# One encoder layer on one core: loads put in the order of use and ahead of stores, gates fetched a step ahead, half of the embedding's products moved behind the mixer

## The chip, the core and the metric

The kernel runs on one core of a Trainium2 chip. The metric is the device time of one execution in microseconds (us); lower is better. TensorE (PE) multiplies into PSUM, VectorE (DVE) and ScalarE (ACT) empty PSUM and prepare operands, and SyncE (SP) issues DMA transfers. Each engine works through its own list of instructions in order, and waits where an operand isn't there.

## What is computed

One layer of an encoder for 512 prompt tokens and 8 sample streams of 16 tokens, 640 tokens in all, with D = 1024 and float32 data:

```python
x = x + 0.5 * swiglu(rms_norm(x), ffn1_w_in, ffn1_w_out)        # d_ff = 2816
z = rms_norm(x) @ w_in_mix                                       # feeds both mixers and the gates
br_ret = (rms_norm(retention(z)) * silu(rg)) @ w_br_ret          # 4 heads, chunks of 64
br_fox = forgetting_attention(z, cached keys and values) @ w_br_fox   # 8 heads of 64, 1024 cached frames
x = x + (sigmoid(g0) * br_ret + sigmoid(g1) * br_fox) @ w_out
x = x + 0.5 * swiglu(rms_norm(x), ffn2_w_in, ffn2_w_out)
x = x + (p @ w_ple) * sigmoid(rms_norm(x) @ w_ple_gate)          # the per-layer embedding, p has 256 columns
```

Keys, values, logits of forgetting and the new retention states are outputs too.

## The kernel before

Activations are held transposed, 128 channels by 640 tokens. Every float32 operand of a large product is split in two fp32r halves: ACT casts the high half (`hi`, L269 for weights, L291 for activations), DVE subtracts it to get the low half (L270, L292). A product is then three matmuls of 128x128 by 320 (or 256) columns, recorded on L205 (L228 are transposes on PE).

*Feed-forward blocks* (`ffn`). The 22 column blocks of d_ff go in groups of 8, 8 and 6. One step f makes one block: two half loads fill a `raw` tile (L535; two raw tiles in turn), its four quarters a11 to a22 enter a scheme of seven products in place of eight (`Seven`), for which DVE adds quarters to each other in place (L403 to L405, L415). The split weights go through rings of six tiles, `wh` for the high and `wl` for the low halves; only a22 goes to other tiles, `blk` (38 of them), so that it may be prepared early:

```python
            self.as_is = Parts().add(a11), Parts().add(a22, spare)
```

After each group its activations are multiplied by w_out, and x is read from DRAM, added to and written back (L591, L592), or, in the last group, handed to the mixer: its normed halves are made on ACT (L469), and x is put into `spill` (L681).

*Mixer.* The input projection, the gates, the embedding's products and the FoX branch are a list of units (`units`); the attention and retention steps are written out between them, and after each of these `fill(us)` lets the list advance by so many modelled microseconds of matmul work. FILL_R is that number for each of the 52 retention steps (4 heads of 13). For each sample, 1024 cached frames of keys and values come in four transfers of 1 MB into four `kv` tiles: K0, K1, V0, V1. Gates (`zdram`) and attention results (`foxd`) go through DRAM. The embedding's products p @ w_ple are four units in the mixer; `embed_take` copies each PSUM tile (L1414) and stores it to `ple` (L1415), from where the last stage reads it.

*Order.* All loads and stores are issued by SP, in the order in which the program issues them, apart from what a scheduler moves when it builds the program; a load waits there for its tile to come free, a store for its data, and what stands behind waits as well. `load` adds a dependency that keeps a transfer from being put too early. On the other engines the scheduler decides the order too; it is fixed before the run.

*Behind the mixer.* The retention branch (eight outputs, gated by a sigmoid on ACT, L1548, and a multiplication on DVE that empties PSUM, L1553), then W_out with its sum into x (L1566) and the second norm, then the second feed-forward block. L442, L444 and L447 are ACT's copies out of PSUM in the scheme of seven products; L1427 and L1430 are sigmoid and multiplication of the FoX branch; L1281 and L1359 are DVE steps of retention, L1347 its silu.

Of the kernel before, what the change touches and what calls it, by code (L numbers as in the profile page):

```python
# [11 lines left out]
F32R = mybir.dt.float32r  # L12
# [7 lines left out]
P = 128  # L20
D = 1024
KC = D // P
# [21 lines left out]

LEAD = 30.0

FILL_P0, FILL_P1, FILL_S0, FILL_S, FILL_R, FILL_B = 1.76, 1.6, 19.8, 10.0, 2.6, 6.4

SM = {}
_at = 0  # L50
# [81 lines left out]
def kernel(  # L132
# [26 lines left out]
    def blk(shape=(P, T), dt=F32, tag="blk"):  # L159
        n = 1  # L160
        for s in shape[1:]:
            n *= s
        assert n <= T
        return bp.tile(list(shape), dt, tag=tag, name=nm(tag), bufs=slots[tag])

    def big(shape=(P, 2048), dt=F32):
        return bp.tile(list(shape), dt, tag="kv", name=nm("kv"), bufs=NKV)
# [44 lines left out]
    def load(out, in_, lead=LEAD):  # L212

        i = nc.sync.dma_start(out, in_)
        at = clock[0] - lead
        name = next((nm_ for c, nm_ in reversed(issued) if c <= at), None)
        if name is not None:
            after(i, name, "no tile taken too soon")
# [171 lines left out]
    class Seven:  # L390
# [8 lines left out]
        def first(self, spare=False):  # L399

            a11, a12, a21, a22 = self.given
            self.as_is = Parts().add(a11), Parts().add(a22, spare)
            nc.vector.tensor_tensor(a11, a21, a11, op=ALU.add)  # L403
            nc.vector.tensor_tensor(a21, a21, a22, op=ALU.add)
            nc.vector.tensor_tensor(a22, a11, a22, op=ALU.add)  # L405
            return self
# [51 lines left out]
    class Norm:  # L458
# [33 lines left out]
        def square(self, xc):  # L492
            if not self.squares:
                self.acc = blk()
                nc.scalar.activation(self.acc, xc, AF.Square)
            else:
                sq = blk()
                nc.scalar.activation(sq, xc, AF.Square)
                nc.vector.tensor_tensor(self.acc, self.acc, sq, op=ALU.add)
            self.squares.append(xc)  # L500
# [19 lines left out]
        def row_stats(self, dsts):  # L520

            t = 0
            for d in dsts:
                for c in range(0, d.shape[1], P):
                    mm(d[:, c:c + P], self.rtok[:, t:t + 1].to_broadcast([P, P]), ident, True, True, skip_group_check=True)
                    t += 1
            self.rb, at = blk(), 0
            for d in dsts:
                nc.scalar.copy(self.rb[:, at:at + d.shape[1]], d)
                at += d.shape[1]  # L530
# [7 lines left out]
    def ffn(xd, norm, w_in, w_o, done, ahead=None, begun=None):  # L538
        pair0 = 0
        for npair in F_GROUPS:  # L540
            acts, pieces, waiting = [], carve(), []

            def act(q, ah, al):
                for hf, sl in enumerate(HALVES):
                    g = tmp()
                    nc.vector.tensor_tensor(g, q.g[hf], norm.rb[:, sl], op=ALU.mult)
                    nc.scalar.activation(g, g, AF.Silu)
                    nc.vector.tensor_tensor(g, g, q.u[hf], op=ALU.mult)
                    split_x(ah[:, sl], al[:, sl], g)

            fs = range(2 * pair0, 2 * (pair0 + npair))
            if ahead and not pair0:
                for step in ahead:
                    ah, al = next(pieces), next(pieces)
                    acts.append((ah, al))
                    step(lambda q: act(q, ah, al))
                fs = fs[len(ahead):]
            q = (begun or Seven(*quarters(up_raw(w_in, fs[0])))).split()
            begun = None
            for f in fs:  # L560
                ah, al = next(pieces), next(pieces)
                acts.append((ah, al))
                if f == 0:
                    for i in range(3):
                        q.product(i, norm.ops, (0, 1, 2))
                    for i in range(3):
                        q.product(i, norm.ops, (3,))
                for i in range(3 if f == 0 else 0, 7):
                    if f == 1 and not ahead and i == 2:
                        sums = bank("pg")  # L570
                        norm.token_stats(sums[:, :TB])
                    if f == 1 and not ahead and i == 4:
                        b0, b1 = bank("pg"), bank("pg")
                        norm.row_stats([b0, b1[:, :P]])
                    q.product(i, norm.ops)
                waiting.append((q, ah, al))
                if f != fs[-1]:
                    q = Seven(*quarters(up_raw(w_in, f + 1))).split()
                while waiting and f > 0:
                    act(*waiting.pop(0))  # L580
            kc = 2 * npair
            for op in range(KC // 2):
                raw = raw_unit(w_o[2 * pair0 * P:2 * (pair0 + npair) * P, op * 256:(op + 1) * 256], kc, 256)
                for o in range(2):
                    xc = blk()
                    load(xc, xd[2 * op + o], 12.0)
                    ps = pair()
                    gemm_t(ps, split_w(raw[:, :, o * P:(o + 1) * P]), acts)
                    for hf, sl in enumerate(HALVES):
                        t = tmp()  # L590
                        nc.vector.scalar_tensor_tensor(t, ps[hf][:, :H2], 0.5, norm.rb[:, sl], op0=ALU.mult, op1=ALU.mult)  # L591
                        nc.vector.tensor_tensor(xc[:, sl], xc[:, sl], t, op=ALU.add)  # L592
                    if pair0 + npair == sum(F_GROUPS):
                        done(xc)
                    else:
                        nc.sync.dma_start(xd[2 * op + o], xc)
            pair0 += npair
# [539 lines left out]
    class Sample:  # L1137
        def __init__(self, b):
            self.b = b

        def loads(self):
            self.k, self.v = [], []
            for to, cache in ((self.k, cache_k), (self.v, cache_v)):
                rows = cache[0, self.b].rearrange("(p j) h d -> p j (h d)", j=8)
                for j in (0, 4):
                    t = big((P, 4, 512))
                    load(t, rows[:, j:j + 4, :], 60.0)
                    to += [t[:, i, :] for i in range(4)]

        def step(self, n):  # L1150

# [259 lines left out]
    def embed_take(q):  # L1411
# [4 lines left out]

        return take

    def fox_begin():
        for pr in range(4):  # L1420
            fox_x.append(parts(fetch(foxd[pr]), blk(dt=F32R), blk(dt=F32R)))

    def fox_take(n0):
        def take(ps, o, hf):
            if hf == 0:
                g = fetch(zdram[Z_G1 + n0 + o])
                nc.scalar.activation(g, g, AF.Sigmoid)  # L1427
                ys.append(g)
            g, sl = ys[n0 + o], HALVES[hf]
            nc.vector.tensor_tensor(g[:, sl], g[:, sl], ps[:, :H2], op=ALU.mult)  # L1430

        return take
# [27 lines left out]
        units[-1].done = lambda hd=hd: ready.add(("rg", hd))  # L1460
    units += units_s(Z_G1, O_ZG + D, 8) + units_s(Z_G0, O_ZG, 8)
    units[-1].begin = embed_begin
    units += [Unit("n", w_ple[0][:, q * 256:(q + 1) * 256], embed_take(q), x=p_x) for q in range(4)]
    units[-2].begin = fox_begin
    ys = []
    units += [Unit("t", w_br_fox[0][:, n * P:n * P + 256], fox_take(n), x=fox_x) for n in range(0, KC, 2)]
    feed = run_units(units)

    credit = [0.0]
# [31 lines left out]
                    fill(FILL_P0 if hu == 0 else FILL_P1)  # L1501
    samples = [Sample(b) for b in range(NB)]
    defer(0.0, sample_new)
    samples[0].loads()
    fill(FILL_B)
    for b in range(NB):
        if b + 1 < NB:
            defer(2.0, samples[b + 1].loads)
        for n in range(8):
            samples[b].step(n)  # L1510
            fill((FILL_S if b else FILL_S0) / 8)
# [28 lines left out]

    y_x, pieces = [], carve()
    ret_x = [parts(fetch(retd[n]), blk(dt=F32R), blk(dt=F32R)) for n in range(KC)]
    for op in range(KC // 2):
        raw = raw_unit(w_br_ret[0][:, op * 256:(op + 1) * 256], KC, 256)
        for o in range(2):
            n = 2 * op + o
            g = fetch(zdram[Z_G0 + n])
            nc.scalar.activation(g, g, AF.Sigmoid)  # L1548
            ps = pair()
            gemm_t(ps, split_w(raw[:, :, o * P:(o + 1) * P]), ret_x)  # L1550
            y = ys[n]
            for hf, sl in enumerate(HALVES):
                nc.vector.tensor_tensor(g[:, sl], g[:, sl], ps[hf][:, :H2], op=ALU.mult)  # L1553
            nc.vector.tensor_tensor(y, y, g, op=ALU.add)
            y_x.append(parts(y, next(pieces), next(pieces)))
    norm2 = Norm(2)
    for op in range(KC // 2):
# [13 lines left out]
        norm2.add_pair(*two)  # L1571
        for xc in two:
            norm2.square(xc)

    norm3 = Norm(3)

# [72 lines left out]
```

## Time and profile before

| | |
|---|---|
| median of 3 runs | 1685.03 us (1680.42 to 1686.94) |
| the profiled execution | 1679.24 us |
| its span, first to last instruction | 1677.5 us |
| TensorE busy | 1644.2 us, 98% |
| VectorE, ScalarE busy | 1177.6 us (70%), 740.4 us (44%) |
| data moved | 248.66 MB, mean 148 GB/s |

The profiled execution is one run with the hardware profiler on; its span leaves out what lies ahead of the first instruction and behind the last. Busy shares are means over stages of very different kinds, so they do not say where an engine waits.

### The profile page before, as it was taken

To read this page: it belongs to the slowest core of one execution; us is meant where nothing else is said; L and a number is where in the kernel's file an instruction comes from. 1 tells how busy PE (TensorE), PEld (TensorE's weight loads), DVE (VectorE), ACT (ScalarE), POOL (GpSimd) and SP (SyncE) were. 2 spreads that over 40 slices of the span, in tenths; PEclk is the share of its full clock that TensorE was granted. 3 is DMA by queue.
4 is the path that set the end of the run, shared out by engine and by line. 5 is a ranking of instruction groups with operands and counts; after the bars stand their busy time and mean duration, and the time that the engine had idled before them with its cause. 6 is when DMAs were issued, how large, how long until landed. Compare 5 with 4: busy or idle time off the path is not lost.

```text
span 1677.5 us, 30453 instructions
## 1 busy us (share of the span) xinstructions
PE 1644.2 (98%) x12073; PEld 1573.0 (94%) x12073; DVE 1177.6 (70%) x2524; ACT 740.4 (44%) x1504; POOL 1.4 (0%) x6
## 2 busy tenths in 40 slices
PE   8999999999999999999999999999999999999999
PEld 7999999999999998888789888899999999999998
DVE  5884787577687746677688866657886588568663
ACT  5552354244455545444434445435553255235442
POOL 0000000000000000000000000000000000000000
PEclk9999999999999999999999999999999999999999
DMA  7134324432542234577774679625234332533343
GB/s 240 51 124 147 107 77 131 154 92 90 164 137 90 86 114 142 205 275 260 270 233 158 223 234 309 230 81 163 81 86 159 121 98 84 171 104 97 112 135 92
DMA packets 228574, 248.66 MB, mean 148 GB/s; under 512 B 15280, under 2 KB 195920, under 8 KB 224336
## 3 DMA queue, kind: packets, MB, share of 16 engines
q1 hardware_dynamic: 228224, 246.64, 45.5%
q8 instruction: 95, 1.56, 0.4%
q14 instruction: 47, 0.39, 0.1%
q10 hardware_dynamic: 208, 0.08, 0.0%
HBM read 198.04 MB, written 48.65 MB: 147 GB/s over the span
## 4 chain that ended last, share of the span: by engine, by line
PE 84%; DMA 8%; DVE 4%; ACT 2%; issue 1%; SPq 0%; ACTq 0%; DVEq 0%
PE pa L205 64%; PE pg L205 16%; PE pa L228 4%; DMA raw<-in_ffn_w_in_dram 3%; DMA blk<-xd 2%; DMA blk<-zdram 1%; DVE wl L270 1%; ACT wh L269 1%; DMA out_dram<-kv 1%; DMA kv<-in_cache_fox_k_dram 1%; DMA blk<-foxd 1%; DMA blk<-in_c_rope_dram 0%; PE pg L228 0%; DVE blk L592 0%; DVE kv L1268 0%
## 5 line engine op out<-in xcount | busy, mean ns | idle before, releaser
L205 PE MATMUL pa<-blk,wh 128*128 128x320 f32 x2672 | 580.1, 311 | 12.4 <-ACT wh L269 5.4
L269 ACT CAST wh<-raw 128x512 fp32r<-128x512 f32 (+1 forms) x566 | 338.3, 613 | 514.9 <-PE pa L205 334.8
L205 PEld LDWEIGHTS pa<-blk,wh 128*128 128x128 f32 x2672 | 440.6, 188 | 21.2 <-ACT wh L269 7.3
L270 DVE TENSOR_TENSOR wl<-raw,wh 128x512 fp32r<-128x512 f32 (+1 forms) x566 | 378.4, 680 | 105.8 <-ACT wh L269 100.2
L205 PE MATMUL pa<-blk,wl 128*128 128x320 f32 x1336 | 393.0, 308 | 0.0
L205 PE MATMUL pa<-kv,wh 128*128 128x320 f32 x1344 | 252.6, 308 | 0.0
L205 PEld LDWEIGHTS pa<-blk,wl 128*128 128x128 f32 x1336 | 246.7, 188 | 0.0
L205 PEld LDWEIGHTS pa<-kv,wh 128*128 128x128 f32 x1344 | 211.1, 188 | 0.0
L205 PE MATMUL pg<-blk,wh 128*128 128x320 f32 x768 | 178.4, 318 | 2.5 <-DVE blk L1430 0.9
L205 PE MATMUL pa<-kv,wl 128*128 128x320 f32 x672 | 153.8, 308 | 0.0
L205 PE MATMUL pg<-wh,blk 128*128 128x256 f32 x768 | 149.7, 290 | 1.5 <-ACT tmp L1414 1.5
L205 PEld LDWEIGHTS pg<-blk,wh 128*128 128x128 f32 x768 | 127.5, 188 | 13.3 <-issue 6.7
L205 PEld LDWEIGHTS pg<-wh,blk 128*128 128x128 f32 x768 | 120.2, 188 | 6.4 <-issue 3.0
L205 PE MATMUL pg<-blk,wl 128*128 128x320 f32 x384 | 119.2, 310 | 0.0
L205 PEld LDWEIGHTS pa<-kv,wl 128*128 128x128 f32 x672 | 112.5, 188 | 0.0
L205 PE MATMUL pg<-wl,blk 128*128 128x256 f32 x384 | 110.0, 287 | 0.0
L591 DVE SCALAR_TENSOR_TENSOR tmp<-pa,blk 128x320 f32<-128x320 f32 x96 | 42.7, 485 | 66.8 <-PE pa L205 66.8
L205 PE MATMUL pa<-wh,blk 128*128 128x256 f32 (+1 forms) x432 | 84.2, 289 | 3.2 <-ACT blk L469 1.8
L205 PE MATMUL pa<-blk,blk 128*128 128x320 f32 (+2 forms) x572 | 87.1, 300 | 0.0
L205 PEld LDWEIGHTS pa<-blk,blk 128*128 128x128 f32 (+1 forms) x572 | 77.4, 179 | 1.3 <-issue 0.6
L205 PEld LDWEIGHTS pg<-wl,blk 128*128 128x128 f32 x384 | 72.3, 189 | 2.5 <-issue 1.7
L205 PEld LDWEIGHTS pg<-blk,wl 128*128 128x128 f32 x384 | 72.2, 188 | 1.4 <-issue 1.4
(257 smaller groups left out, 2112.5 us busy)
## 6 DMA issues: line engine op xcount, KB each, us to landing
raw<-in_ffn_w_in_dram SPq DMA_DIRECT2D x88, 512.0 KB, 4.1
raw<-in_w_in_mix_dram SPq DMA_DIRECT2D x25, 1024.0 KB, 6.5
raw<-in_ffn_w_out_dram SPq DMA_DIRECT2D x16, 1024.0 KB, 5.2
kv<-in_cache_fox_k_dram SPq DMA_DIRECT2D x16, 1024.0 KB, 8.5
kv<-in_cache_fox_v_dram SPq DMA_DIRECT2D x16, 1024.0 KB, 6.5
xd<-blk SPq DMA_DIRECT2D x48, 320.0 KB, 2.9
blk<-xd SPq DMA_DIRECT2D x48, 320.0 KB, 5.7
zdram<-blk SPq DMA_DIRECT2D x32, 320.0 KB, 2.4
```

Source lines behind the costliest of these rows:

```text
L205: i = nc.tensor.matmul(out, lhsT, rhs, start=start, stop=stop, **kw)
L228: tick(nc.tensor.transpose(out, in_, ident[: in_.shape[0], : in_.shape[0]]), 0.11)
L269: nc.scalar.copy(hi, src)
L270: nc.vector.tensor_tensor(lo, src, hi, op=ALU.subtract)
L591: nc.vector.scalar_tensor_tensor(t, ps[hf][:, :H2], 0.5, norm.rb[:, sl], op0=ALU.mult, op1=ALU.mult)
```

## The change

Six edits; the work on the engines stays the same but for two more loads of an activation table on ACT.

1. `ffn` loads x two outputs ahead instead of right ahead of its product.
2. The quarter a11 also goes to `blk` tiles instead of the wh and wl rings. Squares and the row factor of the second norm go to `att` tiles instead of `blk`, and the second block takes its norm's sums in step 0 instead of step 1.
3. The loads of the samples are issued in the order K0 of the next sample, V0 and V1 of this one, K1 of the next; before, all four of the next sample stood together.
4. foxd and the gates of the FoX branch are fetched one unit ahead, and their sigmoid is taken at the start of a unit; the same for the gates of the retention branch.
5. Two of the embedding's four units move from the mixer to the place between W_out and the second block.
6. FILL_R falls from 2.6 to 2.45.

```diff
-FILL_P0, FILL_P1, FILL_S0, FILL_S, FILL_R, FILL_B = 1.76, 1.6, 19.8, 10.0, 2.6, 6.4
+FILL_P0, FILL_P1, FILL_S0, FILL_S, FILL_R, FILL_B = 1.76, 1.6, 19.8, 10.0, 2.45, 6.4
...
-            self.as_is = Parts().add(a11), Parts().add(a22, spare)
+            self.as_is = Parts().add(a11, spare), Parts().add(a22, spare)
...
-                sq = blk()
+                sq = att(shape=(P, T))
...
-            self.rb, at = blk(), 0
+            self.rb, at = blk(tag="att" if self.n == 2 else "blk"), 0
...
-                    if f == 1 and not ahead and i == 2:
+                    if f == 0 and i == 3:
                         sums = bank("pg")
                         norm.token_stats(sums[:, :TB])
-                    if f == 1 and not ahead and i == 4:
+                    if f == 0 and i == 6:
...
+            def fetch_x(n):
+                if n < KC:
+                    coming.append(blk())
+                    load(coming[-1], xd[n], 12.0)
+
+            fetch_x(0)
+            fetch_x(1)
             for op in range(KC // 2):
...
-                    xc = blk()
-                    load(xc, xd[2 * op + o], 12.0)
                     ps = pair()
                     gemm_t(ps, split_w(raw[:, :, o * P:(o + 1) * P]), acts)
+                    fetch_x(2 * op + o + 2)
+                    xc = coming.pop(0)
...
+        def loads(self, then):
+
+            if then:
+                then.load(then.k, cache_k)
+            self.load(self.v, cache_v)
+            self.load(self.v, cache_v)
+            if then:
+                then.load(then.k, cache_k)
...
+    def fox_fetch():
+        fox_x.extend(fetch(foxd[pr]) for pr in range(4))
+
     def fox_begin():
         for pr in range(4):
-            fox_x.append(parts(fetch(foxd[pr]), blk(dt=F32R), blk(dt=F32R)))
+            fox_x[pr] = parts(fox_x[pr], blk(dt=F32R), blk(dt=F32R))
+
+    def gates_fetch(n0):
+
+        if n0 < KC:
+            ys.extend(fetch(zdram[Z_G1 + n0 + o]) for o in range(2))
+
+    def gates_begin(n0):
+        for g in ys[n0:n0 + 2]:
+            nc.scalar.activation(g, g, AF.Sigmoid)
+        gates_fetch(n0 + 2)
...
-    units += [Unit("n", w_ple[0][:, q * 256:(q + 1) * 256], embed_take(q), x=p_x) for q in range(4)]
-    units[-2].begin = fox_begin
+    units += [Unit("n", w_ple[0][:, q * 256:(q + 1) * 256], embed_take(q), x=p_x) for q in range(2)]
+    units[-2].begin = fox_fetch
+    units[-1].begin = lambda: gates_fetch(0)
+    units[-1].middle = fox_begin
...
-        if b + 1 < NB:
-            defer(2.0, samples[b + 1].loads)
+        defer(2.0, lambda: samples[b].loads(samples[b + 1] if b + 1 < NB else None))
...
+    gates = [fetch(zdram[Z_G0 + n]) for n in range(2)]
     for op in range(KC // 2):
         raw = raw_unit(w_br_ret[0][:, op * 256:(op + 1) * 256], KC, 256)
+        for g in gates:
+            nc.scalar.activation(g, g, AF.Sigmoid)
+        g2 = gates
+        gates = [fetch(zdram[Z_G0 + 2 * op + n]) for n in (2, 3)] if op < 3 else []
         for o in range(2):
             n = 2 * op + o
-            g = fetch(zdram[Z_G0 + n])
-            nc.scalar.activation(g, g, AF.Sigmoid)
...
+    raw = raw_unit(w_ple[0][:, 512:], 2, 512)
+    w = [Parts().add(raw[:, :, q * 256:(q + 1) * 256]) for q in range(2)]
+    for q in range(2):
+        for t in range(TB):
+            ps = bank("pg")
+            gemm_n(ps[:, :256], w[q], p_x, t)
+            embed_take(q + 2)(ps, t)
```

*ACT in the first feed-forward block.* `raw_383` holds the weights of one step and `raw_406` those of the next; `blk` and `wh` tiles named from them are their high halves. Before:

```order
L269 CAST wh_384_2329<-raw_383_2326 128x512
L291 CAST kv_352_2085<-tmp_375_2223 128x320
L291 CAST kv_352_2085<-tmp_374_2217 128x320
L442 COPY tmp_379_2256<-pa_378_2243 128x320
L269 CAST blk_409_2476<-raw_406_2469 128x512
L269 CAST wh_388_2340<-raw_383_2326 128x512
L269 CAST wh_390_2344<-raw_383_2326 128x512
```

Of the change:

```order
L269 CAST blk_407_2472<-raw_406_2469 128x512
L291 CAST kv_352_2085<-tmp_375_2223 128x320
L444 COPY tmp_380_2257<-pa_377_2230 128x320
L269 CAST wh_388_2340<-raw_383_2326 128x512
L269 CAST wh_390_2344<-raw_383_2326 128x512
L269 CAST blk_409_2476<-raw_406_2469 128x512
L269 CAST wh_392_2348<-raw_383_2326 128x512
```

In both a cast from the next step's `raw_406` stands in front of `wh_388`, which is of this step; it was a22's (`blk_409`) and is now a11's (`blk_407`), and a22's follows two casts later.

*SP between samples 5 and 6.* `kv_1862` (not shown) and `kv_1863` are K0 and K1 of sample 5. Before, `kv_1864` and `kv_1865` are its V0 and V1, and `kv_1933` is K0 of sample 6:

```order
L214 DMA kv_1863_9195<-in_cache_fox_k_dram 128x2048
L784 DMA zdram_5111<-blk_1942_9522 128x640
L214 DMA kv_1864_9197<-in_cache_fox_v_dram 128x2048
L787 DMA zdram_5111<-blk_1939_9500 128x640
L249 DMA raw_1978_9691<-in_w_in_mix_dram 128x8x256
L214 DMA kv_1865_9199<-in_cache_fox_v_dram 128x2048
L214 DMA kv_1933_9479<-in_cache_fox_k_dram 128x2048
L1238 DMA foxd_5115<-tmp_1970_9656 128x4x16
```

Of the change, where `kv_1863` is K1 of sample 5, `kv_1931` and `kv_1934` are K0 and K1 of sample 6, and `kv_1932` and `kv_1933` V0 and V1 of sample 5:

```order
L214 DMA kv_1863_9195<-in_cache_fox_k_dram 128x2048
L792 DMA zdram_5111<-blk_1940_9518 128x640
L795 DMA zdram_5111<-blk_1937_9496 128x640
L214 DMA kv_1931_9475<-in_cache_fox_k_dram 128x2048
L249 DMA raw_1976_9687<-in_w_in_mix_dram 128x8x256
L214 DMA kv_1932_9477<-in_cache_fox_v_dram 128x2048
L214 DMA kv_1933_9479<-in_cache_fox_v_dram 128x2048
L1254 DMA foxd_5115<-tmp_1968_9652 128x4x16
L214 DMA kv_1934_9481<-in_cache_fox_k_dram 128x2048
```

K0 of sample 6 has gone from behind both halves of the values to ahead of them.

*SP between W_out and the second feed-forward block.* `xd1` are stores of x, `spill` its loads. Before, `raw_2835` holds the weights of the block's second step:

```order
L214 DMA blk_2760_13573<-spill_446 128x640
L214 DMA blk_2767_13636<-spill_446 128x640
L1567 DMA xd1_87<-blk_2760_13573 128x640
L535 DMA raw_2835_14017<-in_ffn2_w_in_dram 128x8x128 x2
L1567 DMA xd1_87<-blk_2767_13636 128x640
```

Of the change, these are `raw_2865`:

```order
L1598 DMA xd1_87<-blk_2767_13632 128x640
L1598 DMA xd1_87<-blk_2774_13695 128x640
L1431 DMA ple_5113<-tmp_2799_13804 128x256
L1431 DMA ple_5113<-tmp_2801_13814 128x256
L1431 DMA ple_5113<-tmp_2803_13824 128x256
L1431 DMA ple_5113<-tmp_2805_13834 128x256
L1431 DMA ple_5113<-tmp_2807_13844 128x256
L1431 DMA ple_5113<-tmp_2809_13854 128x256
L535 DMA raw_2865_14180<-in_ffn2_w_in_dram 128x8x128
L1431 DMA ple_5113<-tmp_2811_13864 128x256
L1431 DMA ple_5113<-tmp_2813_13874 128x256
L535 DMA raw_2865_14180<-in_ffn2_w_in_dram 128x8x128
```

The weights of the second step have gone from between two stores of x to behind the last of them and six of the moved stores of the embedding, their second half behind eight.

## Rows read from the trace of the kernel before

**Rows 1.** The page: span, and busy time of the engines

```profile
span 1677.5 us, 30453 instructions
PE 1644.2 (98%) x12073; PEld 1573.0 (94%) x12073; DVE 1177.6 (70%) x2524; ACT 740.4 (44%) x1504; POOL 1.4 (0%) x6
```

**Rows 2.** Waits of PE: for whom; us in total, times, longest

```profile
PE pa L205 <- ACT wh L269: 5.4, 6, 1.6
...
PE pa L228 <- DMA kv<-in_cache_fox_k_dram: 3.3, 1, 3.3
PE pa L205 <- DVE blk L1553: 2.4, 1, 2.4
PE pa L205 <- ACT blk L469: 1.8, 1, 1.8
PE pa L205 <- ACT tmp L444: 1.6, 1, 1.6
PE pg L205 <- ACT tmp L1414: 1.5, 2, 1.1
...
PE pa L205 <- DVE att L1281: 1.3, 1, 1.3
...
PE pg L205 <- DVE blk L1430: 0.9, 1, 0.9
PE pa L205 <- DVE blk L1359: 0.8, 1, 0.8
```

**Rows 3.** The same from 50 to 470 us, then from 1195 to 1620

```profile
PE pa L205 <- ACT wh L269: 3.0, 3, 1.4
...
PE pa L205 <- ACT wh L269: 2.3, 3, 1.6
```

**Rows 4.** Waits of ACT

```profile
ACT blk L269 <- DMA raw<-in_ffn_w_in_dram: 57.5, 30, 5.1
...
ACT blk L291 <- DMA blk<-foxd: 6.0, 3, 2.5
```

**Rows 5.** Timeline of SP, ACT and PE, 354 to 364: start, duration [idle before]

```profile
355.39 2.01 SPq L535 DMA_DIRECT2D raw<-in_ffn_w_in_dram  x2
...
362.21 0.62 ACT L269 CAST blk<-raw 128x512 fp32r<-128x512 f32 x1 [3.14 <-DMA raw<-in_ffn_w_in_dram]
...
363.40 0.85 PE L205 MATMUL pa<-blk,wh 128*128 128x320 f32 x4 [1.41 <-ACT wh L269]
```

**Rows 6.** Windows: PE busy (count), granted clock, DMA share, GB/s

```profile
300.00:350.00 50.00, 50.00 (x344) 1.00 0.48 154
```

**Rows 7.** The page, DMA issues: count, KB each, median us to landing

```profile
raw<-in_ffn_w_in_dram SPq DMA_DIRECT2D x88, 512.0 KB, 4.1
```

**Rows 8.** The chain that ended last, 420 to 470: start, us, what

```profile
458.25 0.32 SPq L681
458.66 3.51 DMA blk<-xd
...
464.08 5.95 PE pa L205 x34
```

**Rows 9.** Windows of PE at the start of the mixer, columns as in rows 6

```profile
464.08:468.00 3.92, 3.92 (x19) 0.56 1.08 369
468.00:472.00 4.00, 4.00 (x35) 1.00 0.68 213
```

**Rows 10.** Timeline of SP, 780 to 812

```profile
790.81 0.33 SPq L214 DMA_DIRECT2D kv<-in_cache_fox_v_dram  x1
...
797.42 0.33 SPq L214 DMA_DIRECT2D kv<-in_cache_fox_k_dram  x1
```

**Rows 11.** Windows in the sample stage, columns as in rows 6

```profile
785.00:790.00 5.00, 5.00 (x39) 1.00 0.13 49
```

**Rows 12.** Timeline of ACT, 1040 to 1049

```profile
1043.92 0.35 ACT L1310 COPY tmp<-pa 128x256 f32<-128x256 f32 x1
1044.29 1.28 ACT L1347 ACT_TABLE_LOAD   x1
1045.58 0.74 ACT L1347 ACTIVATE blk<-blk 128x640 f32<-128x640 f32 x1
```

More of the change, by code (lines that the diff above doesn't have):

```diff
@@ L580, in ffn @@
                     act(*waiting.pop(0))
-            kc = 2 * npair
+            kc, coming = 2 * npair, []
+            def fetch_x(n):
[4 more added lines that the diff above has]
+            fetch_x(1)
             for op in range(KC // 2):
@@ L1139, in __init__, with load @@
             self.b = b
-        def loads(self):
             self.k, self.v = [], []
[L1143 to L1148, printed above, removed]
+        def load(self, to, cache):
+            j, t = len(to), big((P, 4, 512))
+            load(t, cache[0, self.b].rearrange("(p j) h d -> p j (h d)", j=8)[:, j:j + 4, :], 60.0)
+            to += [t[:, i, :] for i in range(4)]
+        def loads(self, then):
[5 more added lines that the diff above has]
+                then.load(then.k, cache_k)
         def step(self, n):
@@ L1417, in embed_take @@
         return take
+    def fox_fetch():
+        fox_x.extend(fetch(foxd[pr]) for pr in range(4))
     def fox_begin():
         for pr in range(4):
-            fox_x.append(parts(fetch(foxd[pr]), blk(dt=F32R), blk(dt=F32R)))
+            fox_x[pr] = parts(fox_x[pr], blk(dt=F32R), blk(dt=F32R))
[6 more added lines that the diff above has]
+        gates_fetch(n0 + 2)
     def fox_take(n0):
         def take(ps, o, hf):
-            if hf == 0:
-                g = fetch(zdram[Z_G1 + n0 + o])
-                nc.scalar.activation(g, g, AF.Sigmoid)
-                ys.append(g)
             g, sl = ys[n0 + o], HALVES[hf]
@@ L1462 @@
     units[-1].begin = embed_begin
-    units += [Unit("n", w_ple[0][:, q * 256:(q + 1) * 256], embed_take(q), x=p_x) for q in range(4)]
-    units[-2].begin = fox_begin
+    units += [Unit("n", w_ple[0][:, q * 256:(q + 1) * 256], embed_take(q), x=p_x) for q in range(2)]
+    units[-2].begin = fox_fetch
+    units[-1].begin = lambda: gates_fetch(0)
+    units[-1].middle = fox_begin
     ys = []
-    units += [Unit("t", w_br_fox[0][:, n * P:n * P + 256], fox_take(n), x=fox_x) for n in range(0, KC, 2)]
+    units += [Unit("t", w_br_fox[0][:, n * P:n * P + 256], fox_take(n), begin=lambda n=n: gates_begin(n), x=fox_x)
+              for n in range(0, KC, 2)]
     feed = run_units(units)
@@ L1503 @@
     defer(0.0, sample_new)
-    samples[0].loads()
+    samples[0].load(samples[0].k, cache_k)
+    samples[0].load(samples[0].k, cache_k)
     fill(FILL_B)
     for b in range(NB):
-        if b + 1 < NB:
-            defer(2.0, samples[b + 1].loads)
+        defer(2.0, lambda: samples[b].loads(samples[b + 1] if b + 1 < NB else None))
         for n in range(8):
@@ L1542 @@
     ret_x = [parts(fetch(retd[n]), blk(dt=F32R), blk(dt=F32R)) for n in range(KC)]
+    gates = [fetch(zdram[Z_G0 + n]) for n in range(2)]
     for op in range(KC // 2):
         raw = raw_unit(w_br_ret[0][:, op * 256:(op + 1) * 256], KC, 256)
+        for g in gates:
+            nc.scalar.activation(g, g, AF.Sigmoid)
+        g2 = gates
+        gates = [fetch(zdram[Z_G0 + 2 * op + n]) for n in (2, 3)] if op < 3 else []
         for o in range(2):
             n = 2 * op + o
-            g = fetch(zdram[Z_G0 + n])
-            nc.scalar.activation(g, g, AF.Sigmoid)
             ps = pair()
             gemm_t(ps, split_w(raw[:, :, o * P:(o + 1) * P]), ret_x)
-            y = ys[n]
+            y, g = ys[n], g2[o]
             for hf, sl in enumerate(HALVES):
```

## Prediction

> **What bounds the kernel now.** I read the page's totals first. TensorE (PE) is busy 1644.2 us of a span of 1677.5 us, and VectorE and ScalarE are far below that [rows 1]. The change leaves the number of matmuls as it is, so what it can win lies in the 33.3 us in which PE stands still. The second view, the waits of PE, says for whom it stood: 5.4 us in six waits for the fp32r cast of a weight (line 269), 3.3 us for one transfer of cached keys, 2.4 us for the multiplication that empties PSUM in the retention branch (L1553), 1.8 us for the normed input of the mixer (L469), 1.6 us for a copy in the first step of the second feed-forward block (L444), 1.5 us for the embedding's copies (L1414), 0.9 us for the FoX branch (L1430), and 1.3 and 0.8 us in retention steps (L1281, L1359) [rows 2]. By stretch the six weight casts are 3.0 us in the first feed-forward block and 2.3 us in the second [rows 3]. So the kernel is bound by PE, and the change has to be judged by which of these waits it ends and which it starts.
>
> **Feed-forward weights.** ScalarE works in order. In the rows of its order ahead of this text, the cast `blk<-raw` of the next step, which needs that step's transfer, stands in front of `wh_388`, which this step's product needs. ScalarE stood 57.5 us in 30 such places [rows 4]; PE feels the few where the transfer is issued late. In one of them the transfer was issued at 355.39, the cast of the next step started at 362.21, and PE got its weight at 363.40 after 1.41 us of waiting [rows 5]. A matmul of 320 columns takes 145 ns (50.0 us for 344) [rows 6]. In the order of the program before, 55 matmuls lie between the one that frees the raw buffer and the one that waits: 55 × 0.145 = 8.0 us, plus the 1.4 us of waiting, so the chain needs 9.4 us. The change puts the quarter a11 into blk tiles too, five casts for each step in the ring of six instead of six, and the buffer is freed earlier: the same place has 71 matmuls, 10.3 us, and the wait goes. In the first block the other distances are 67 to 79 (one of 59), so I take its whole 3.0 us. In the second block five places have 61 or 62, 8.9 us, of which a chain of 9.4 us would leave 0.5 us each and a shorter one nothing; the transfer here landed 6.8 us after its issue, against a median of 4.1 us [rows 7]. I take 1.0 of the 2.3 us. Together **−4.0** (bounds 0 and −5.4).
>
> **Loads of x ahead of stores.** In the last output products of the first block the chain runs through SP: the spill of one x issued at 458.25, and only behind it the load of the next at 458.66, 3.51 us to land; the product started at 464.08 [rows 8]. Loads two outputs ahead take that transfer out; PE's 1.8 us go, since the vector work that remains lies under the next group's matmuls. The row shows a second price: over the 3.92 us from 464.08 the granted clock was 0.56, that is for most of it the lower of its two levels (1.2 GHz), after PE had stood for that wait; 19 matmuls ran there and 35 in the next 4.00 us [rows 9]. At the later pace 19 take 2.2 us, so 1.7 us more are lost. **−3.5** (bounds −1.8 and −3.5).
>
> **Sample loads.** The first keys of sample 6 were issued at 797.42, because their buffer held values of sample 4 until then; the buffer of the first keys of sample 5 was free at 790.81, when its values were issued into it [rows 10]. SP's rows ahead of this text show the keys taking that place, two loads forward. With 6.6 us more they land ahead of the 3.3 us wait. The DMA engines had room: from 785 to 790 us they were busy 0.13 of the time [rows 11]. **−3.3** (bounds 0 and −3.3). What is late next is the second half of the values, first read after the softmax of the sample that they belong to; a whole sample of matmuls covers it.
>
> **Gates and foxd a step ahead.** The embedding's copies waited on ScalarE behind casts of foxd (6.0 us in three places [rows 4]), whose loads stand on SP behind the embedding's stores; fetched a unit ahead and cast later, they are out of the way, and half of the stores are gone from there: −1.5 − 0.9 = **−2.4** (bounds 0 and −2.4). In the retention branch the sigmoid, now issued at the start of a step, stands ahead of the weight casts, and L1553's **−2.4** goes (bounds 0 and −2.4). Two more table loads are added. In the row one takes 1.28 us: the copy before ends at 1044.27, the load starts at 1044.29, and the next activation at 1045.58 [rows 12]. ScalarE is 44% busy, so I charge **+0.6** of 2 × 1.28 = 2.6 us (bounds 0 and +2.6).
>
> The Trainium skill, in "ScalarE: Activation LUTs", section "What ACT_TABLE_LOAD costs", puts a switch at 1283 ns and a drain of about 1380 ns, 2.66 us in all. Here the trace agrees with the load and shows no drain beside it. By the page the two loads would cost up to 5.3 us, and my charge would double to 1.2 us.
>
> **Embedding products moved.** Two units, 60 matmuls of 256 columns, leave the mixer for the place between W_out and the second block: no more than 60 × 0.145 = 8.7 us of work [rows 6], not lost but moved. There it covers the last pair's norm, for which PE waits at L444: **−1.6** (bounds 0 and −1.6). It brings ten stores onto SP, and SP's rows show `raw_2865`, the weights of the second step, behind six to eight of them. From the matmul whose product the last store ahead holds to the first that needs the weights lie 42 matmuls, 6.1 us at most. The chain from issue to use was 8.0 us in one case [rows 5], and would be 5.3 us with the median landing [rows 7]. So a new wait between 0 and 1.9 us; I take **+1.2**, nearer to the slow one, because stores run beside it.
>
> In retention 52 steps (4 heads of 13) each get 0.15 us less matmul work to fill them, 7.8 us in all. If every step were bound by its own chain, all of it would turn into waiting; now only two waits there, 1.3 and 0.8 us, reach PE [rows 2], so most steps have slack. I take **+1.5** (bounds 0 and +7.8).
>
> **Sum.** −4.0 − 3.5 − 3.3 − 2.4 − 2.4 − 1.6 = −17.2; +0.6 + 1.2 + 1.5 = +3.3; together −13.9 us. The profiled execution took 1679.24 us, 1.7 more than its span, which gives 1665.3. It lies 5.8 us below the median of 1685.03, so on the median I predict 1671 us.
>
> **The rivals.** *Given back*: the costs come at their bounds. 7.8 + 1.9 + 2.6 = 12.3 against 17.2 leaves −4.9, or 1680 us. For it speaks that retention already shows two waits; against it that SP, ScalarE and VectorE all have room in those stretches. *The order of loads decides nothing*: transfers would be held by buffers and by the DMA engines, not by what stands ahead on SP. Then −3.5, −3.3 and −2.4 fall away, and −8.0 + 3.3 = −4.7 gives 1680 us. Against it: the load was issued right behind a store [rows 8], and the DMA engines were idle shortly before the keys [rows 11]. *Slower*: now two casts `blk<-raw` of the next step stand in ScalarE's order instead of one. If each of the 44 feed-forward steps (88 half loads [rows 7]) paid one more cast of 0.62 us [rows 5] on PE, that is +27.3, and 1671 becomes 1698 us. It decides from (13.9 + 8.4) / 44 = 0.5 us for each step on. Against it: the distances grew in nearly every step.
>
> **How the numbers follow.** About 0.5% of the time, 8.4 us, can be told from no change. The forecast, −9 to −19, has 0.62; given back 0.22; order decides nothing 0.09; slower 0.07. So faster 0.62, same 0.31, slower 0.07. The low end is all gains at their bounds and no costs, −18.6, less 3.3 us for half the spread of the three runs: 1663, and I say 1662. The high end is either of the two rivals at 1680 us and the same 3.3 us: 1684 with rounding. Above it lies the slower case, and what is left below is for gains that I do not see.
>
> **What would show it.** Right: the waits of PE lose the kv row, L1553, L469 and the L1414 row; weight casts fall from 5.4 to about 1.5 us; the granted clock at the start of the mixer stays at 1.00. Wrong in the costs: PE waits for L1281, L1359 or other retention lines sum to well over 3.6 us, or a wait for line 269 over 1.9 us stands at the start of the second block. Wrong in the gains: the keys or x still appear as waits. The whole is wrong if the six weight waits become dozens.

## The result, and the profile after

The change takes 1668.70 us (median of 4 runs, 1668.46 to 1669.05) against 1684.28 us before (four runs; the 1685.03 us of the table ahead of the prediction is the median of the first three): a ratio of 0.9909, with a 95% interval of 0.989 to 0.9929. The profiled execution took 1668.46 us. One execution behind the times below, of the run with a11 back in the weight rings, was slow (2301.47 us at a mean granted clock of 0.655) and is left out of that run's figures. The page of the changed kernel, span and engines:

```profile
span 1666.4 us, 30484 instructions
PE 1648.0 (99%) x12073; PEld 1575.3 (95%) x12073; DVE 1172.2 (70%) x2524; ACT 743.6 (45%) x1506; POOL 1.4 (0%) x6
```

Against [rows 1] the span is 11.1 us shorter, and PE stands still for 18.4 us instead of 33.3. So its idle time fell by 14.9 us, but its busy time rose by 3.8 us with the same 12073 matmuls. All waits of its PE, columns as in [rows 2]:

```profile
PE pa L228 <- DMA kv<-in_x_prompt_dram: 5.1, 1, 5.1
PE pg L205 <- DVE blk L788: 1.9, 1, 1.9
PE pg L205 <- ACT tmp L1430: 1.6, 1, 1.6
PE pg L228 <- DVE tmp L1642: 1.4, 1, 1.4
PE pa L205 <- ACT blk L348: 1.2, 1, 1.2
PE pa L205 <- DVE tmp L546: 1.0, 1, 1.0
PE pa L205 <- ACT tmp L444: 0.9, 1, 0.9
PE pa L205 <- ACT wh L269: 0.8, 1, 0.8
PE pa L205 <- ACT tmp L1430: 0.3, 1, 0.3
```

The rows of L348, L546 and `in_x_prompt` belong to the first 50 us and stand in both kernels. Gone are the keys (3.3 us), the retention branch's multiplication that empties PSUM (2.4), the mixer's normed input (1.8), both retention steps (2.1), all six weight casts (5.4) and the copy at the start of the second block (1.6). New are L1642 in the last stage, an L444 of 0.9 us later in the second block (at 1396 us), and one weight cast at its start. L1430 is now the embedding's copy, L1414 before; PE waits 1.9 us for it in two waits, where it waited 1.5. L788, which makes a gate of the input projection, is L780 of the kernel before, which had a shorter wait there:

```profile
PE pg L205 <- DVE blk L780: 0.6, 1, 0.6
```

The weight cast stands in the place that the prediction named. Timeline of SP, ACT and PE there, columns as in [rows 5]:

```profile
1172.66 0.38 SPq L535 DMA_DIRECT2D raw<-in_ffn_w_in_dram  x1
...
1177.13 0.62 ACT L269 CAST blk<-raw 128x512 fp32r<-128x512 f32 x1 [1.66 <-DMA raw<-in_ffn_w_in_dram]
...
1178.32 0.56 PE L205 MATMUL pa<-blk,wh 128*128 128x320 f32 x2 [0.76 <-ACT wh L269]
```

The first half of the second step's weights is issued behind six stores of the embedding, and PE gets its weight 5.7 us later.

The waits do not say everything. The lines that take the keys' transposes out of PSUM, and those that add W_out's product to x, date the stages. Before (count, durations, first and last start):

```profile
L1168 DVE COPY att<-pa x32: 678/692/693, 666.9 to 845.9; 128x512 f32<-128x512 f32 x32
...
L1566 DVE TENSOR_TENSOR blk<-blk,pa x16: 478/482/487, 1129.5 to 1178.5; 128x320 f32<-128x320 f32 x16
```

After:

```profile
L1184 DVE COPY att<-pa x32: 677/690/692, 660.5 to 841.5; 128x512 f32<-128x512 f32 x32
...
L1597 DVE TENSOR_TENSOR blk<-blk,pa x16: 477/479/489, 1113.6 to 1163.0; 128x320 f32<-128x320 f32 x16
```

The samples begin 6.4 us earlier, but their last copy only 4.4 us earlier: 181.0 us from first to last instead of 179.0, though the wait for the keys is gone. (In the second profile of the kernel before, at the end of the experiments, they go from 665.1 to 845.7, 180.6 us.) W_out begins 15.9 us earlier, of which up to 8.7 us are the products moved behind it.

The reason for the longer sample stage stands in PE's timeline. Four pairs of heads have their scores made by matmuls that use 32 columns of the array each, and run side by side if they follow one another; each is recorded twice, so that a block has eight records. One such block of the changed kernel (start, duration, count):

```profile
731.99 1.05 PE L205 MATMUL pa<-att,blk 128*32 128x512 f32 x4
732.97 0.66 PE L228 MATMUL pa<-sm,kv 128*128 128x128 f32 x4
733.56 1.05 PE L205 MATMUL pa<-att,blk 128*32 128x512 f32 x4
```

And its counterpart in the kernel before:

```profile
737.53 1.07 PE L205 MATMUL pa<-att,blk 128*32 128x512 f32 x8
```

Whole, the eight records take 1.0 us to the next matmul; split by four transposes of the next sample's keys, 0.98 us each time, so one such split costs about a microsecond. The order of the programs, in which the scheduler puts these transposes, has 10 of 16 blocks whole before and 5 after, and so have the traces. Not every split costs that much: three blocks before and two after are interrupted only by products of the values, also 32 columns wide, and take 1.06 us. Matmuls of 128 columns stand inside three blocks before and nine after. In all, counted from each record's start to the next one's and without waits, the scores take 19.4 us before and 24.0 us after.

### The profile page after: what moved, and what is told of

Read it like the earlier page. It is cut to its first block, busy times and chain, and to the rows that moved or that the text cites. A ratio compares the mean times of both kernels' runs of the same rounds, so it can differ in the third digit from the quotient of the medians.

```text
span 1666.4 us, 30484 instructions
## 1 busy us (share of the span) xinstructions
PE 1648.0 (99%) x12073; PEld 1575.3 (95%) x12073; DVE 1172.2 (70%) x2524; ACT 743.6 (45%) x1506; POOL 1.4 (0%) x6
## 4 chain that ended last, share of the span: by engine, by line
PE 96%; DMA 3%; DVE 1%; ACT 0%; issue 0%; SPq 0%; DVEq 0%; ACTq 0%
PE pa L205 73%; PE pg L205 19%; PE pa L228 4%; DMA raw<-in_ffn_w_in_dram 1%; DMA kv<-zdram 1%; DMA out_dram<-kv 0%; DMA zdram<-blk 0%; DMA tmp<-ple 0%; PE pg L228 0%; ACT wh L269 0%; DVE wl L270 0%; DVE tmp L1642 0%; ACT tmp L1637 0%; DVE kv L1397 0%; DVE tmp L1638 0%
## 5 line engine op out<-in xcount | busy, mean ns | idle before, releaser
L269 ACT CAST wh<-raw 128x512 fp32r<-128x512 f32 (+1 forms) x525 | 316.0, 613 | 489.8 <-PE pa L205 291.8
L205 PE MATMUL pa<-blk,wh 128*128 128x320 f32 x2344 | 512.2, 311 | 3.8 <-ACT blk L348 1.2
L270 DVE TENSOR_TENSOR wl<-raw,wh 128x512 fp32r<-128x512 f32 (+1 forms) x525 | 351.4, 678 | 93.3 <-ACT wh L269 88.3
L205 PEld LDWEIGHTS pa<-blk,wh 128*128 128x128 f32 x2344 | 388.0, 189 | 11.9 <-issue 2.8
L205 PE MATMUL pa<-blk,wl 128*128 128x320 f32 x1172 | 343.9, 309 | 0.0
L205 PEld LDWEIGHTS pa<-blk,wl 128*128 128x128 f32 x1172 | 216.0, 188 | 0.0
L205 PE MATMUL pa<-blk,blk 128*128 128x320 f32 (+2 forms) x1064 | 167.1, 304 | 0.0
L205 PEld LDWEIGHTS pa<-blk,blk 128*128 128x128 f32 (+1 forms) x1064 | 151.4, 183 | 2.0 <-PE pa L205 1.2
L270 DVE TENSOR_TENSOR blk<-raw,blk 128x512 fp32r<-128x512 f32 x82 | 56.4, 688 | 54.7 <-ACT blk L269 33.6
L269 ACT CAST blk<-raw 128x512 fp32r<-128x512 f32 x82 | 50.6, 621 | 80.1 <-DMA raw<-in_ffn_w_in_dram 63.3
```

Of the source, the lines that this page charges most:

```text
L205: i = nc.tensor.matmul(out, lhsT, rhs, start=start, stop=stop, **kw)
L269: nc.scalar.copy(hi, src)
L270: nc.vector.tensor_tensor(lo, src, hi, op=ALU.subtract)
```

## The experiments

Each run is of the kind "undo one part of the change", "one part alone", or "a rule added". Medians are compared with the change's 1668.70 us; where it matters, the ratio to the kernel before on the same chip stands beside them, since the old kernel's own median moved between 1680.1 and 1684.3 us from one set of runs to the next. For the same reason the length of a stage in the traces is given where it decides.

**Undo the order of the sample loads.**

```diff
-            if then:
-                then.load(then.k, cache_k)
-            self.load(self.v, cache_v)
-            self.load(self.v, cache_v)
-            if then:
-                then.load(then.k, cache_k)
+            for s in then:                     # all four of the next sample
+                s.load(s.k, cache_k)
+                s.load(s.k, cache_k)
+                s.load(s.v, cache_v)
+                s.load(s.v, cache_v)
```

> The change with the old order of the sample loads (all four of the next sample together). If the early keys only saved the 3.3 us wait, as the prediction has it, this costs 3.3 us: 1672.0. If they also split blocks of scores that ran side by side (10 whole blocks of 16 in the order with the old loads, 5 with the new; about 0.98 us for each split one), 4.9 us come back with it: about 1667, with the kv wait of 3.3 us in the trace and more blocks of four scores in 0.99 us.

It took 1665.03 us (1661.55 to 1666.37; ratio 0.9904, 0.9876 to 0.9932). The wait for the keys is back with 3.0 us, and the blocks are whole as before. Span and median are 3 to 4 us under the change's; by the ratios the two cannot be told apart. The sample stage, by the copies of the keys, takes 180.6 us against 181.0, so what differs in the medians lies behind it. Either way the 3.3 us that the early keys save do not reach the end; no run of the kernel before with the new loads alone was made.

**Keep the blocks of a sample whole.** Only the order on PE is constrained: the transposes of keys, the four scores and the products of the values are each a block, and the blocks follow one another as the program issues them.

```diff
+    blocks = []
+
+    def whole(insts):
+        if blocks:
+            after(insts[0], blocks[-1], "one block of a sample after the other")
+        blocks.append(insts[-1].ins.name)
...
+                        ms.append(m)
+                    whole(ms)
```

> The change with one more rule on the order alone: the blocks of a sample (transposes of keys, four scores, values) follow one another on TensorE in the order of the program, which makes 13 of 16 score blocks whole instead of 5. If split blocks cost 0.98 us each: 8 x 0.98 = 7.8 us less, about 1661. If what looks slow in a split block is hidden elsewhere: 1668.7, no change.

1659.25 us (1658.49 to 1660.33), ratio 0.9875 (0.9853 to 0.9896): 9.4 us less than the change and faster than both kernels. The block that was split, in this kernel's timeline, has its transposes ahead of it:

```profile
729.26 0.60 PE L228 MATMUL pa<-sm,kv 128*128 128x128 f32 x4
729.79 1.06 PE L205 MATMUL pa<-att,blk 128*32 128x512 f32 x8
```

The copies of the keys date the stage, columns as above:

```profile
L1192 DVE COPY att<-pa x32: 677/683/693, 660.2 to 833.2; 128x512 f32<-128x512 f32 x32
```

That is 173.0 us, 8.0 less than in the change. It agrees with the 7.8 us expected, but in part by luck: two of the blocks that became whole had cost hardly anything when split (1.06 us against 0.97), and the scores alone take 18.4 us, 5.5 less than in the change. The rule holds transposes and values together as well; that the other 2.5 us come from that was not tried.

**The same rule with the old sample loads**, and **the same rule in the kernel before**.

> The rule on the order of sample blocks together with the old order of the sample loads. It weighs the early keys alone, with the score blocks kept whole in both. If the keys are worth the 3.3 us wait, as the prediction has it: 3.3 us over the run with the rule and the new loads, less about 1 us for each block that is whole here and not there, so 1660 to 1663. If they are worth nothing once blocks are whole: 1659 or less.

> The kernel before with the rule on the order of sample blocks: 15 score blocks whole instead of 10. If a split block costs 0.98 us in the old kernel too: 4.9 us less than before. If the split ones are hidden behind the wait for keys there: no change.

The first took 1668.54 us (1667.03 to 1671.56; ratio 0.992), 9.3 us over the rule with the new loads and outside both expectations; the second 1685.50 us (1683.30 to 1687.39; ratio 1.0012, 1.0001 to 1.0023), no gain. With whole blocks PE arrives at the late keys sooner and stands there longer: the transposes that wait for them start at 801.3 us here and at 801.7 with the old loads and split blocks. Waits of PE, the rule with the old loads:

```profile
PE pa L228 <- DMA kv<-in_cache_fox_k_dram: 6.9, 2, 6.1
```

And its granted clock around that wait, columns as in [rows 6]:

```profile
790.00:800.00 10.00, 5.25 (x73) 0.93 1.04 396
800.00:806.00 6.00, 4.67 (x20) 0.54 0.30 123
```

The stage, dated as above:

```profile
L1191 DVE COPY att<-pa x32: 677/691/694, 659.7 to 841.7; 128x512 f32<-128x512 f32 x32
```

So by the medians early keys are worth 9.3 us where the blocks stay whole, and whole blocks are worth 9.4 us where the keys are early; by the ratios 0.45% of the time, 7.6 us, and 0.34%, 5.7 us; by the stage in the traces 9.0 and 8.0 us. Each alone gives nothing.

**Undo the loads of x ahead**, and **these loads alone in the kernel before**.

```diff
-                    fetch_x(2 * op + o + 2)
+                    fetch_x(2 * op + o)        # right ahead of its product
```

> The change with x loaded right ahead of its product, as before. By the prediction 3.5 us come back (1.8 us of waiting for L469 at the start of the mixer and 1.7 us at the lower granted clock behind it): 1672. If the order of loads and stores decides nothing: 1668.7 and no wait for L469.

> The kernel before with only x loaded two outputs ahead. By the prediction 3.5 us less than before on the same chip, no wait for L469 and the granted clock at 1.00 behind 464 us. If, as undoing the edit in the change suggests, it is worth about 0.8 us: no change that can be measured, and a part of the wait stays.

The first took 1669.45 us (1669.27 to 1669.96), 0.75 us more; by the ratios, 0.9935 (0.9914 to 0.9956) against 0.9909 (0.989 to 0.9929), it is 4.4 us with intervals that overlap, so the whole time does not weigh it. Waits of PE from 440 to 480 us:

```profile
PE pa L205 <- ACT blk L469: 0.9, 2, 0.8
```

The second took 1682.09 us against 1683.55, ratio 0.9993 (0.9984 to 1.0003): no change that can be measured. But its trace has no wait of PE from 440 to 480 us, and the granted clock did not fall:

```profile
464.00:468.00 4.00, 4.00 (x35) 1.00 0.84 228
```

So the loads ahead suffice to end wait and clock loss, and without them the rest of the change ends part of it too. The traces weigh the place itself: 120 matmuls of 264 columns open the mixer, and 80 of them have these rows, the kernel before, these loads in it, the change, and the change without them (durations, first and last start):

```profile
L205 PE MATMUL pa<-wh,blk x80: 278/284/422, 459.9 to 479.1; 128*128 128x264 f32 x80
L205 PE MATMUL pa<-wh,blk x80: 278/284/369, 460.3 to 476.0; 128*128 128x264 f32 x80
L205 PE MATMUL pa<-wh,blk x80: 279/284/369, 456.7 to 472.3; 128*128 128x264 f32 x80
L205 PE MATMUL pa<-wh,blk x80: 278/284/391, 457.3 to 474.4; 128*128 128x264 f32 x80
```

They take 19.2 and 15.7 us in the kernel before, 15.6 and 17.1 us in the change: the loads ahead are worth 3.5 us there and 1.5 us here. In the second profile of the kernel before, where the clock did not fall at this place, they take 17.8 us, and the loads ahead are worth 2.1 us.

**Undo a11 in blk tiles.**

```diff
-            self.as_is = Parts().add(a11, spare), Parts().add(a22, spare)
+            self.as_is = Parts().add(a11), Parts().add(a22, spare)
```

> The change with a11 back in the weight rings. By the prediction the waits for weight casts come back, 5.4 us against 0.8: about 1673. If something else ended them (the norm's sums one step earlier, squares in other tiles): under 1 us more, 1669.

1674.16 us (1672.19 to 1679.32), ratio 0.9959 (0.9942 to 0.9976): 5.5 us back. The weight casts among its waits of PE:

```profile
PE pa L205 <- ACT wh L269: 5.3, 7, 1.6
```

**Undo the gates and foxd ahead in the FoX branch.**

```diff
-    units[-2].begin = fox_fetch
-    units[-1].begin = lambda: gates_fetch(0)
-    units[-1].middle = fox_begin
+    units[-1].begin = fox_begin                # loads and casts together
...
+            if hf == 0:                        # in fox_take
+                g = fetch(zdram[Z_G1 + n0 + o])
+                nc.scalar.activation(g, g, AF.Sigmoid)
+                ys.append(g)
```

> The change with foxd and the FoX branch's gates fetched where they are used, as before. By the prediction 2.4 us come back: 1671, with waits for the embedding's copies behind foxd and for the FoX multiplication. If the waits only changed owner (the trace of the change has 1.9 us for the embedding's copies and 1.9 for a gate product there): 1668.7 or less.

1676.52 us (1676.01 to 1677.86), 7.8 us more, which neither expectation has. The wait is one that neither kernel has, for retention's multiplication with its silu gate (L1376), whose gate came late:

```profile
PE pa L205 <- DVE blk L1376: 4.9, 1, 4.9
```

ScalarE made that gate (L1363) after standing idle for its load:

```profile
1013.18 0.74 ACT L1363 ACTIVATE blk<-blk 128x640 f32<-128x640 f32 x1 [6.28 <-DMA blk<-zdram]
```

The window around it:

```profile
1010.00:1025.00 15.00, 10.07 (x38) 0.77 1.03 377
```

**Undo the embedding's move, with FILL_R at 2.6.** The products behind W_out fall away, and `range(2)` is `range(4)` again.

> The change with all four embedding units in the mixer and FILL_R at 2.6, as before. By the prediction's terms (-1.6 for L444, +1.2 and +1.5) the edit costs 1.1 us, so undoing it gives about 1667.6. If instead the move ended the retention waits (L1281, L1359, 2.1 us) and shortened the stretch with the embedding, undoing it costs 3 to 5 us: 1672 to 1674, with L444 at about 1.6 us again.

1681.57 us, ratio 0.9991: 12.9 us more, far over both expectations, and all but the whole gain lost. Its waits of PE:

```profile
PE pg L205 <- ACT tmp L1430: 5.2, 2, 4.8
...
PE pa L205 <- ACT tmp L1430: 1.8, 1, 1.8
```

The window around them:

```profile
1010.00:1025.00 15.00, 10.20 (x47) 0.66 1.03 361
```

The embedding's copies stand on ScalarE behind two silus of retention (L1363), one of the sigmoids that are now issued earlier (L1449) and a table load for each kind, from 1014.52 to 1019.65 us; PE waits for PSUM meanwhile, and the granted clock falls. What the expectation had for L444 did not come: of the waits in the first step of the second block, from 1183 to 1215 us, only this is left:

```profile
PE pa L205 <- DVE pa L448: 0.5, 1, 0.5
```

**Undo FILL_R alone.**

```diff
-FILL_P0, FILL_P1, FILL_S0, FILL_S, FILL_R, FILL_B = 1.76, 1.6, 19.8, 10.0, 2.45, 6.4
+FILL_P0, FILL_P1, FILL_S0, FILL_S, FILL_R, FILL_B = 1.76, 1.6, 19.8, 10.0, 2.6, 6.4
```

> The change with FILL_R at 2.6 and the embedding's units moved all the same. By the prediction thinner filling costs 1.5 us (0 to 7.8), so this gives about 1667. If retention has slack with 2.45 as well, and the units only last less long here: 1668.7 or more, with new waits behind the last unit.

1684.45 us, ratio 1.0004: 15.8 us more, so the second expectation holds. Its waits of PE that neither kernel has:

```profile
PE pa L205 <- ACT blk L291: 5.9, 2, 5.7
...
PE pa L205 <- DVE ty L333: 4.2, 1, 4.2
```

The end of retention and what follows:

```profile
1045.00:1090.00 45.00, 34.45 (x213) 0.89 0.49 167
```

The last units of the list are the FoX branch's (multiplication L1455), and retention ends with the multiplications of L1376. First here, then in the change:

```profile
L1455 DVE TENSOR_TENSOR blk<-blk,pg x16: 478/489/490, 1004.6 to 1046.2; 128x320 f32<-128x320 f32 x16
L1376 DVE TENSOR_TENSOR blk<-blk,pa x8: 278/280/283, 919.8 to 1057.8; 128x128 f32<-128x128 f32 x8
...
L1455 DVE TENSOR_TENSOR blk<-blk,pg x16: 475/484/489, 1006.5 to 1049.7; 128x320 f32<-128x320 f32 x16
L1376 DVE TENSOR_TENSOR blk<-blk,pa x8: 277/277/279, 913.5 to 1046.2; 128x128 f32<-128x128 f32 x8
```

With two units fewer and the old number the list of matmul work is used up 11.6 us before retention ends, and its last steps stand bare; in the change the list outlasts retention by 3.5 us.

**Undo the gates ahead in the retention branch.** Fetch and sigmoid go back into the loop over outputs.

> The change with the retention branch's gates fetched and their sigmoid taken output by output, as before. By the prediction the wait for the multiplication that empties PSUM comes back, 2.4 us: 1671. If the embedding's move or another edit ended it: 1668.7.

1668.22 us (1667.66 to 1671.38): no difference, and no wait there.

**The kernel before once more**, unchanged.

> The kernel before once more, for a second profile. If the spread of its runs (1676 to 1688 us) comes from the granted clock falling behind its long waits in some executions, this profile shows the same waits as the first and the lower level of the clock behind other ones. If the waits themselves differ, it shows another length for the keys or the weights.

1682.11 us (1680.29 to 1685.89), the profiled execution 1680.35, 1.1 us over the first. Its profile has the same waits within 0.6 us, the keys with 3.2. What differs is the clock, above all at two places and in opposite ways. At the start of the mixer, where [rows 9] has 0.56, and behind the keys, where the first profile has 1.00, it has

```profile
464.08:468.00 3.92, 3.92 (x35) 1.00 1.09 345
...
806.00:810.00 4.00, 4.00 (x20) 0.57 0.08 35
```

## Why the prediction was right, and where its steps were not

The total held: 1671 was said and 1668.70 measured, faster by 0.9%. Several of its terms did not, and their errors cancelled, so the closeness is in part luck. One premise beneath them failed: "what it can win lies in the 33.3 us in which PE stands still". The idle time fell by 14.9 us, but the busy time rose by 3.8 us, where by the clock at the start of the mixer alone it should have fallen by 1.7.

*Feed-forward weights*, −4.0: right. All 5.4 us of waiting went, with 0.8 us new at a place priced under the embedding's move, and undoing a11 alone brings 5.5 us back. It was somewhat too small: the five places of the second block with 61 or 62 matmuls did not wait at all, so the chain there is shorter than the 9.4 us of [rows 5].

*Loads of x*, −3.5: wait and clock loss did go, and the loads alone suffice for it; at the place itself 3.5 us went. Of these the 1.7 us of the clock belong to one execution: behind a wait of 1.5 us at the same place the second profile keeps 1.00. As the worth of this edit in the change the term is too large, 1.5 us at the place and 0.75 us in the medians, since the other edits end part of the same wait. Which of them does was not tried.

*Sample loads*, −3.3: the wait went, the time did not. The step that failed is "what is late next ... a whole sample of matmuls covers it". Nothing was late; with the keys loaded earlier the scheduler put the next transposes between the scores, and the scores take 4.6 us more. With the old order of loads they take 19.4 us again.

*Gates and foxd ahead*, −2.4: 0.5 us of it came. The waits changed owner, as the rival *given back* would have it in this place, with the embedding's copies of now (L1430, 1.6 and 0.3 us) for L1414 and L1430 of before (2.4 us). The step that failed is "they are out of the way": a cast of foxd still waits for its load ahead of the copies, and the sigmoid's table load, charged with 0.6 us together with another, stands ahead of the copy that PE waits for. (L788, 1.9 us at 930 us, is not of this edit: with it undone 1.4 us stay.) ACT of the change:

```profile
989.16 0.72 ACT L291 CAST blk<-blk 128x640 fp32r<-128x640 f32 x1 [1.85 <-DMA blk<-foxd]
...
993.80 1.28 ACT L1449 ACT_TABLE_LOAD   x1
995.10 0.74 ACT L1449 ACTIVATE blk<-blk 128x640 f32<-128x640 f32 x1
995.74 0.35 ACT L1430 COPY tmp<-pg 128x256 f32<-128x256 f32 x1
```

The granted clock right behind, from 998 to 1002 us:

```profile
998.00:1002.00 4.00, 3.77 (x11) 0.57 1.06 340
```

*Retention branch*, −2.4: the wait ended, but its own edit is not needed for that: without it the wait stays ended. The same holds for every other part that was undone alone; which of them end it together was not settled.

*Embedding's move*, −1.6 and +1.2: the second is right. The wait for the second step's weights came, with 0.8 us of the 0 to 1.9 said, and is absent where the move is undone. The wait for L444 at the start of the second block went too, but not because the products cover the last pair's norm: with the move undone 0.5 us of waiting stand there, and none for L444. What ended it stays open; the second edit changes this step too, where the second block takes its norm's sums, and was undone only for a11.

*Thinner filling*, +1.5: the sign was wrong. Less work in each step made the list last to the end of retention, and 2.6 with the shorter list costs 15.8 us. Both retention waits went, and they are back with 1.2 us at 2.6; why the thinner filling ends them was not tried. I had asked what each step loses and not when the list ends. The two edits are one, and with the gates ahead they are three: undone one at a time they cost 12.9, 15.8 and 7.8 us, in sum more than twice what the whole change gains.

*The basis*, +5.8 us from the profiled execution to the median: it does not carry over. In profiled executions I forecast 1665.3 us and 1668.46 came, 3.1 us too fast; the offset of 5.8 us hid that, because the changed kernel's runs lie within 0.6 us of its profile. The 5.8 us were not a property of the old kernel's profile: its second profiled execution took 1680.35 us in a set of runs with a median of 1682.11. Both profiles show the lower clock behind waits, each behind another one, and they differ by 1.1 us; what spreads its other runs from 1676 to 1688 us is not shown.

The rival *order decides nothing* is refuted for x, by the stage in the traces, and for the keys, where blocks are whole; *slower* by the feed-forward steps, of which none waits for a weight any more but the second of the second block.

## What to carry to other kernels

Price an earlier load also by what the scheduler will put into the time that it opens, and read the order of the engine that waited. Where hand-set filling feeds a stage, ask when the list of work runs out before asking what each step gets. Edits to such a stage belong together, and undoing them one by one does not give their shares.

## What the runs showed of the hardware

Matmuls on 32 columns of the array ran four at a time when they followed one another: eight records took 1.0 us in one block and 2 × 0.98 us when matmuls of 128 columns stood between. Products of the values, also on 32 columns, in the same place left a block at 1.06 us.

The granted clock fell behind waits of 1.8 us [rows 9] and 3.2 us to 0.56 and 0.57 for some 4 us, that is for most of it to the lower of its two levels (1.2 GHz). The same wait of the same kernel was followed by 1.00 in one execution and 0.57 in another (the keys), and by 0.56 in one and 1.00 in another (the start of the mixer). The change repeated within 0.6 us, and without its x loads ahead within 0.7. Kernels with late keys spread over 4.1 us and more, but so did some with early keys (7.1 us with a11 back in the rings), so the keys do not explain the spread.
